# Five raw buffers, loads six blocks ahead, gate reads in four parts and a one-hot copied by ScalarE, in a decoder block with a 16,384-expert mixer

## The chip, the cores and the metric

The kernel runs on one core of a Trainium2 chip. The metric is the device time of one execution in microseconds. Three runs before the change took 1752.38, 1755.32 and 1758.9 us; the median is 1755.32 us. Of the two programs one execution more is profiled with the hardware profiler; that of the kernel before took 1750.83 us.

Engines are named as in the profile: PE (matrix multiply), DVE (VectorE), ACT (ScalarE), POOL (GpSimd), SP (SyncE, which issues most of the DMAs). Each works through its own list of instructions strictly in order.

## The reference

One decoder layer on 512 tokens of width 1024, in float32. The first half (state-space branch, sliding-window attention, gates, output projection) is not touched by the change. The second half is a product-key mixture of single-neuron experts:

```python
q = (xt @ w_query).reshape(t, PEER_HEADS, 2, PEER_KEY_DIM // 2)
s = jnp.einsum('thkd,hknd->thkn', q, sub_keys)
vals, idx = lax.top_k(s, PEER_TOPK)
cand = vals[:, :, 0, :, None] + vals[:, :, 1, None, :]      # 16 x 16 candidates per head
best, pos = lax.top_k(cand.reshape(t, PEER_HEADS, 256), PEER_TOPK)
expert = i1 * N_SUB_KEYS + i2                               # i1, i2 looked up by pos
gate = jax.nn.softmax(best, axis=-1)
a = einsum('cd,ced->ce', x, u_tab[expert])
w = gate * gelu(a)
out = einsum('ce,ced->cd', w, v_tab[expert])
```

Every token has 8 heads x 16 experts = 128 experts out of 16,384, and each expert is one row of 1024 numbers of the table `peer_u` and one of `peer_v`.

## The kernel before, in words

The kernel does the expert mixer in two ways at once.

**The dense way, for tokens 128 to 511.** Both tables are read whole, as 128 blocks of 128 experts each. A *U block* multiplies 128 rows of `peer_u` with the 384 tokens and applies gelu; a *V block* multiplies the weights (gelu times gate, zero where a token does not choose the expert) with 128 rows of `peer_v` and sums into six banks of PSUM that stay open to the end. Each product is made of three matrix products (`mm3`, and the like of it in `v_mm`): every float32 operand is split into a high part `hi` (cast to float32r on ACT, L123) and a low part `lo` (the difference, on DVE, L124), and hi·hi, hi·lo and lo·hi are summed. So a block of either table costs: one load of 512 KB into a `t_raw` buffer (issued by SP, L1120 or L1122), one cast on ACT, one subtraction on DVE, and 24 matmuls of 384 columns (`a_mm`, L93 to L95) or 18 of 512 columns (`v_mm`, L1156 to L1159) on PE. The result of a U block is evicted from PSUM by a gelu on ACT (L1132).

**The sparse way, for tokens 0 to 127.** `sparse_tile` gathers 256 rows, 128 of each table, with one expert per token in each gather (POOL, L1188, 512 KB each), and works each off on DVE in one instruction, L1205 for a row of `peer_u` and L1207 for one of `peer_v`. It is a generator that the main loop advances a little at each block.

**Gates.** Which expert a token takes is found on DVE (`topk`, for four tiles of 128 tokens). For the three dense tiles `gate_matrix` then makes the full table of gates, 384 tokens x 16,384 experts, as products of two one-hot matrices. For eight tokens at a time (a *gate step*, 48 in all) DVE makes four tiles of 128 x 1024 fp16: `ol` (which of 128 second indices, L1105), `oh` and `ol` (times the high and low part of the gate, L1106 and L1107) and `one` (which of 128 first indices, L1108). `ol`, `oh` hold the token as their innermost index; `one` holds it as the outer one, since its rows are what PE loads. One step later PE multiplies them (16 matmuls, L1091 and L1092), ACT evicts the result into `g_st`, and each 16 tokens ACT's queue writes 1 MB of `g_st` to the tensor `G_d` in DRAM. Later SP reads the gates of eight V blocks back in one DMA of 1536 KB (`v_g<-G_d`, L1136), two buffers in turn. All 24 writes of `G_d` come before the first of these reads.

**The order.** The table stages are one loop over `order`. Its first `ALONE` entries are U blocks, then V blocks come with the rest of the U blocks spread between them, one after about every third V block. As the list is built, one U block more stands ahead of the first V block, so 91 U blocks come first in the kernel before, and 37 U and 128 V blocks after. At place *i* the loop issues: the load of the block 4 places on (`table_load`), the split of the block 2 places on (`unit_split`), in the V stage also the read of gates, the read-back of a U result and the preparation of the weights (`w_prep`, L1145, L88, L89), then the block's matmuls, and then background work: `RATE_A` units of top-k and gate work (until it is done; it must be done ten blocks before `ALONE`), and `RATE_S` (before the V stage) or `RATE_V` (in it) units of the sparse way, 1.2 units to a row. DVE's and POOL's lists follow this order as it is written (`manual_schedule`). The lists of PE, ACT and SP are set by the framework's scheduler, which places instructions by its own estimate of when their inputs and buffers are free.

**Buffers.** Three `t_raw` buffers and three pairs `hi`/`lo` (`WB`). A load waits until the subtraction L124 has freed its buffer; a cast waits until PE has done with the `hi` of three blocks before. U results stay in SBUF while there is room: `RES` = 15 tiles `A_first`, and 20 tiles `A_mid` in the memory that the top-k frees tile by tile; the others go to DRAM (`A_d<-u_g`, L1353, issued by ACT, 192 KB) and come back in the V stage (`v_a<-A_d`, L1337, issued by SP). 54 of the 128 do.

**Semaphores of DMAs.** The framework hands out eight DMA semaphores in turn to every DMA that SP or ACT issues. A DMA whose semaphore was last given to another one waits, on the engine that issues it, until that other DMA has landed.

Of the kernel before, what the change touches and what calls it, by code (L numbers as in the profile page):

```python
# [10 lines left out]
F32 = mybir.dt.float32  # L11
# [47 lines left out]
class Builder:  # L59
    RATE_A, RATE_S, RATE_V, RATE_G = 2.4, 0.72, 1.44, 6.0  # L60
    ALONE = 90
    G0, S5C, G1, RATE_Q = 0, 70.0, 8.0, 3.0
# [6 lines left out]
    POOL_U, POOL_R = 2, (0,)  # L69
    RES, WB, SOLO = 15, (3, 3), 2.0  # L70

# [988 lines left out]
    def gate_matrix(self, pool, i12, gate, Gd, tile_no, cost=1.25):  # L1060
# [38 lines left out]
        for t1 in range(0, 128, TB):  # L1099
            tb = slice(t1, t1 + TB)  # L1100
            sh = [128, 128, TB]
            wide = lambda a: a[:, None, tb].to_broadcast(sh)
            oh, ol = (mk(sh, n, F16, bufs=2) for n in ("oh", "ol"))
            one = mk([128, TB, 128], "one", F16, bufs=2)
            nc.vector.tensor_tensor(ol, self.iota16, wide(iT[:, 1, :]), op=ALU.is_equal)  # L1105
            nc.vector.tensor_mul(oh, ol, wide(gh))  # L1106
            nc.vector.tensor_mul(ol, ol, wide(gl))  # L1107
            nc.vector.tensor_tensor(one, self.iota1[:, None, :].to_broadcast([128, TB, 128]),  # L1108
                                    iT[:, 0, tb, None].to_broadcast([128, TB, 128]), op=ALU.is_equal)
            if late:  # L1110
                multiply(*late)
            late = (t1, one, oh, ol)
            yield cost
        multiply(*late)

    def table_load(self, u):

        raw = self.wb.tile([128, D], F32, tag="raw", name=self.nm("t_raw"), bufs=self.WB[0])
        if u < 128:
            self.nc.sync.dma_start(out=raw.rearrange("p (k e) -> p k e", e=128), in_=self.i["peer_uT"][u])  # L1120
        else:
            self.nc.sync.dma_start(out=raw, in_=self.i["peer_v"][(u - 128) * 128:(u - 127) * 128, :])  # L1122
        return raw
# [9 lines left out]

    def g_load(self, pool, b, Gd):
        g = pool.tile([128, Gd.shape[0], self.GB, self.TS], F32, tag="v_g", name=self.nm("v_g"), bufs=2)
        self.nc.sync.dma_start(out=g, in_=Gd[:, :, b:b + self.GB, :].rearrange("g p b t -> p g b t"))  # L1136
        return g

# [72 lines left out]
    def run(self, out):  # L1211
# [4 lines left out]
        with ExitStack() as fs:  # L1216
# [86 lines left out]
            rows = L(fs, "rows")  # L1303
            A1 = L(fs, "ares1").tile([128, N1, DT], F32, name="A_first")
            free[:0] = [A1[:, n, :] for n in range(N1)]
            sparse = self.sparse_tile(sq, rows, xrow, ef0, gate0, hd[0], out[0])
# [13 lines left out]
            def ahead(i, n):  # L1320
                return order[i + n] if 0 <= i + n < len(order) else (2, 0)

            with tc.manual_schedule(engines={ET.DVE, ET.Pool}):
                for i in range(-4, len(order)):
                    v, b = ahead(i, 4)
                    if v < 2:
# [3 lines left out]
                    if vp:  # L1330
                        v, b = ahead(i, 8)
                        if v == 1 and b % self.GB == 0:
                            gg[b] = self.g_load(vp, b, Gd)
                        v, b = ahead(i, 4)
# [48 lines left out]
    def consts(self, pool):  # L1383
# [6 lines left out]
        self.iota16 = pool.tile([128, 128, 8], F16, name="iota16")  # L1390
        self.iota1 = pool.tile([128, 128], F16, name="iota1")
        nc.gpsimd.iota(self.iota1, pattern=[[1, 128]], base=0, channel_multiplier=0, allow_small_or_imprecise_dtypes=True)
        nc.gpsimd.iota(self.iota16, pattern=[[1, 128], [0, 8]], base=0, channel_multiplier=0, allow_small_or_imprecise_dtypes=True)
# [67 lines left out]
```

## Time and profile before

| | |
|---|---|
| median of three runs | 1755.32 us (1752.38 to 1758.9) |
| the profiled execution | 1750.83 us, of which the span of the trace is 1748.8 us |
| PE, DVE, ACT, POOL busy | 1631.2, 1444.8, 751.0, 580.2 us |
| first U block on PE | 527.4 us after the span's start |
| first V block on PE | 1038.4 us |
| 24 writes of `G_d`, 16 reads `v_g` | 1024 KB and 1536 KB each |
| mean DMA rate over the span | 243 GB/s |

Times in the views count from the span's start. A row of a group of instructions reads: line, engine, operation, output<-input, shapes, count, then busy time, the mean duration of one in ns, and the idle time of the engine just before, with what ended most of it. In the rows by stretch of time, each engine has its busy time and, in brackets, its number of instructions; then come the granted TensorE clock, the busy share of the DMA engines, and GB/s. In rows in order of time, the brackets at the end hold the idle time before the row and what ended it. "SPq" and "ACTq" are DMAs being issued on SP and ACT. Matmuls overlap in the trace (each starts before the one ahead has ended), so the pace of PE is read from the distance between starts.

### The profile page before, as it was taken

How to read it: one execution, taken by the hardware profiler on the slowest of the kernel's cores; microseconds unless marked ns; L12 is line 12 of the kernel's file. 1: busy time of each engine (PE TensorE's matmuls, PEld its weight loads, DVE VectorE, ACT ScalarE, POOL GpSimd, SP SyncE). 2: the span in 40 equal slices, each digit the busy share in tenths (PEclk: the TensorE clock that was granted, in tenths of full speed). 3: DMA queues.
4: the chain of work that ended last, by engine and by line, in shares of the span. 5: the costliest groups of instructions: out<-in, count | busy, mean ns of one | idle time of the engine just before them, and what ended most of it. 6: DMA issues, size and time to landing. Idle time of an engine off the chain costs nothing.

```text
span 1748.8 us, 24910 instructions
## 1 busy us (share of the span) xinstructions
PE 1631.2 (93%) x8831; PEld 1429.4 (82%) x8831; DVE 1444.8 (83%) x2931; ACT 751.0 (43%) x1242; POOL 580.2 (33%) x473
## 2 busy tenths in 40 slices
PE   7789999898999898898899799999999999999998
PEld 5568878786899888898889798888888888888776
DVE  6799778897798999999999467878777777778776
ACT  5256656565563434434444233333333333333332
POOL 2562123333521111111112143544444444444441
PEclk9899999999999999899999899999999999999999
DMA  7823452656744456666668988989999999999885
GB/s 227 150 85 97 151 169 84 169 164 190 232 138 164 161 207 235 223 223 238 243 227 303 348 302 299 313 314 322 330 328 340 320 321 334 336 323 324 285 289 195
DMA packets 231501, 424.10 MB, mean 243 GB/s; under 512 B 16160, under 2 KB 148304, under 8 KB 228304
## 3 DMA queue, kind: packets, MB, share of 16 engines
q1 hardware_dynamic: 171680, 237.97, 41.4%
q0 software_dynamic: 36864, 134.23, 21.2%
q10 hardware_dynamic: 22832, 50.30, 8.9%
q8 instruction: 69, 1.13, 0.3%
q14 instruction: 56, 0.46, 0.1%
HBM read 370.94 MB, written 51.51 MB: 242 GB/s over the span
## 4 chain that ended last, share of the span: by engine, by line
PE 45%; DVE 26%; DMA 8%; issue 4%; ACT 2%; SPq 2%; POOL 0%; ACTq 0%; DVEq 0%; POOLq 0%
PE po L1156 9%; PE po L1157 9%; PE po L1159 8%; DVE lo L124 6%; PE pa L93 4%; PE pa L95 4%; PE pa L94 4%; DMA t_raw<-peer_uT 3%; DVE g_one L1108 3%; DVE sp_row L1205 3%; DMA t_raw<-peer_v 2%; DVE g_oh L1106 2%; DVE g_ol L1105 1%; ACT hi L123 1%; SPq L1337 1%
## 5 line engine op out<-in xcount | busy, mean ns | idle before, releaser
L123 ACT CAST hi<-t_raw 128x1024 fp32r<-128x1024 f32 x256 | 269.1, 1051 | 461.4 <-PE pa L94 148.4
L93 PE MATMUL pa<-x2h,hi 128*128 128x384 f32 x1024 | 353.2, 345 | 36.9 <-ACT u_g L1132 25.8
L124 DVE TENSOR_TENSOR lo<-t_raw,hi 128x1024 fp32r<-128x1024 f32 x256 | 312.4, 1221 | 88.6 <-ACT hi L123 88.1
L1188 POOL DMA_INDIRECT sp_row<-peer_u,sp_ei x128 | 199.3, 1557 | 528.3 <-DVE sp_row L1205 489.0
L95 PE MATMUL pa<-x2h,lo 128*128 128x384 f32 x1024 | 349.2, 343 | 13.3 <-DVE lo L124 13.2
L94 PE MATMUL pa<-x2l,hi 128*128 128x384 f32 x1024 | 348.0, 340 | 0.0
L1156 PE MATMUL po<-hi,v_wh 128*128 128x512 f32 x768 | 304.6, 397 | 5.9 <-ACT v_wh L88 5.9
L1157 PE MATMUL po<-lo,v_wh 128*128 128x512 f32 x768 | 303.4, 395 | 0.0
L1188 POOL DMA_INDIRECT sp_row<-peer_v,sp_ei x128 | 195.6, 1528 | 273.2 <-DVE sp_acc L1207 240.9
L93 PEld LDWEIGHTS pa<-x2h,hi 128*128 128x128 f32 x1024 | 196.1, 192 | 47.1 <-ACT u_g L1132 29.7
L1159 PE MATMUL po<-hi,v_wl 128*128 128x512 f32 x768 | 228.7, 395 | 0.0
L95 PEld LDWEIGHTS pa<-x2h,lo 128*128 128x128 f32 x1024 | 195.8, 191 | 19.4 <-DVE lo L124 18.5
L94 PEld LDWEIGHTS pa<-x2l,hi 128*128 128x128 f32 x1024 | 196.1, 191 | 1.7
L1156 PEld LDWEIGHTS po<-hi,v_wh 128*128 128x128 f32 x768 | 144.3, 188 | 41.9 <-ACT v_wh L88 8.9
L1159 PEld LDWEIGHTS po<-hi,v_wl 128*128 128x128 f32 x768 | 143.8, 187 | 35.4
L1157 PEld LDWEIGHTS po<-lo,v_wh 128*128 128x128 f32 x768 | 144.3, 188 | 32.7
L1207 DVE SCALAR_TENSOR_TENSOR sp_acc<-sp_row,sp_a,sp_acc 128x1024 f32<-128x1024 f32 x128 | 163.7, 1279 | 1.0 <-DMA sp_row<-peer_v,sp_ei 0.7
L1205 DVE SCALAR_TENSOR_TENSOR sp_row<-sp_row,xrow 128x1024 f32<-128x1024 f32 x128 | 155.7, 1216 | 4.5 <-DMA sp_row<-peer_u,sp_ei 4.5
L89 DVE TENSOR_TENSOR v_wl<-v_w,v_wh 128x384 fp32r<-128x384 f32 x128 | 71.5, 558 | 103.2 <-ACT v_wh L88 103.2
L88 ACT CAST v_wh<-v_w 128x384 fp32r<-128x384 f32 x128 | 65.5, 512 | 211.2 <-DVE v_w L1145 211.0
L123 ACT CAST hi<-raw 128x1024 fp32r<-128x1024 f32 x88 | 92.0, 1048 | 87.0 <-PE gps L94 15.5
L124 POOL TENSOR_TENSOR lo<-raw,hi 128x1024 fp32r<-128x1024 f32 x28 | 70.0, 2499 | 117.3 <-ACT hi L123 117.3
(455 smaller groups left out, 2912.4 us busy)
## 6 DMA issues: line engine op xcount, KB each, us to landing
t_raw<-peer_uT SPq DMA_DIRECT2D x128, 512.0 KB, 4.3
t_raw<-peer_v SPq DMA_DIRECT2D x128, 512.0 KB, 4.9
G_d<-g_st ACTq DMA_DIRECT2D x24, 1024.0 KB, 5.7
v_g<-G_d SPq DMA_DIRECT2D x16, 1536.0 KB, 14.6
raw<-w_in SPq DMA_DIRECT2D x32, 512.0 KB, 4.2
A_d<-u_g ACTq DMA_DIRECT2D x54, 192.0 KB, 3.9
v_a<-A_d SPq DMA_DIRECT2D x54, 192.0 KB, 7.2
raw<-w_ab SPq DMA_DIRECT2D x64, 128.0 KB, 3.6
```

Source lines behind the costliest of these rows:

```text
L89: self.nc.vector.tensor_sub(lo, src, r32(hi))
L93: mm(out, lh, rh, start=first, stop=False)
L94: mm(out, lh, rl, start=False, stop=False)
L95: mm(out, ll, rh, start=False, stop=last)
L123: self.nc.scalar.copy(hi, raw)
L124: (self.nc.gpsimd if pool_lo else self.nc.vector).tensor_sub(lo, raw, r32(hi))
L1156: mm(po[j][i], wh[:, c], hi[:, hs[i]], start=first, stop=False)
L1157: mm(po[j][i], wh[:, c], lo[:, hs[i]], start=False, stop=False)
L1159: mm(po[j][i], wl[:, c], hi[:, hs[i]], start=False, stop=last)
L1188: nc.gpsimd.indirect_dma_start(out=got[k], out_offset=None, in_=self.i[n], in_offset=bass.IndirectOffsetOnAxis(ap=ei[:, s:s + 1], axis=0))
L1205: nc.vector.scalar_tensor_tensor(r, r, 1.0, xrow, op0=ALU.mult, op1=ALU.mult, accum_out=av[:, s:s + 1])
L1207: nc.vector.scalar_tensor_tensor(acc, r, av[:, s:s + 1], acc, op0=ALU.mult, op1=ALU.add)
```

## The change

- `table_load` takes its buffers from two pools: of every five loads in turn three go to the old three buffers and two to a new pool `wx` with two. Loads are issued six places ahead (`FAR`), where it was four.
- To make room, `RES` falls from 15 to 9. 68 U results go through DRAM where 54 did.
- The read of gates for eight V blocks is issued as four DMAs of 384 KB (`PARTS`), 8, 7, 6 and 5 places ahead of their first use, where it was one DMA of 1536 KB 8 places ahead.
- `one` is made in two steps: DVE makes `o1` with the token innermost (as `ol` is), and ACT copies it into `one` with the token as the outer index.
- `ALONE` is 96 where it was 90, and the rates of the background work are 2.2, 0.96 and 1.36 where they were 2.4, 0.72 and 1.44 (`RATE_A`, `RATE_S`, `RATE_V`).
- The constant `iota1` goes.

```diff
-    RATE_A, RATE_S, RATE_V, RATE_G = 2.4, 0.72, 1.44, 6.0
-    ALONE = 90
+    RATE_A, RATE_S, RATE_V, RATE_G = 2.2, 0.96, 1.36, 6.0
+    PARTS = 4
+    ALONE, MORE, FAR = 96, 2, 6
...
-    RES, WB, SOLO = 15, (3, 3), 2.0
+    RES, WB, SOLO = 9, (3, 3), 2.0
...
             one = mk([128, TB, 128], "one", F16, bufs=2)
+            o1 = mk(sh, "o1", F16, bufs=2)
+            nc.vector.tensor_tensor(o1, self.iota16, wide(iT[:, 0, :]), op=ALU.is_equal)
+            nc.scalar.copy(one, o1.rearrange("p b t -> p t b"))
             nc.vector.tensor_tensor(ol, self.iota16, wide(iT[:, 1, :]), op=ALU.is_equal)
             nc.vector.tensor_mul(oh, ol, wide(gh))
             nc.vector.tensor_mul(ol, ol, wide(gl))
-            nc.vector.tensor_tensor(one, self.iota1[:, None, :].to_broadcast([128, TB, 128]),
-                                    iT[:, 0, tb, None].to_broadcast([128, TB, 128]), op=ALU.is_equal)
...
-        raw = self.wb.tile([128, D], F32, tag="raw", name=self.nm("t_raw"), bufs=self.WB[0])
+        self.loads += 1
+        pool, n = (self.wb, self.WB[0]) if self.loads % (self.WB[0] + self.MORE) < self.WB[0] else (self.wx, self.MORE)
+        raw = pool.tile([128, D], F32, tag="raw", name=self.nm("t_raw"), bufs=n)
...
-    def g_load(self, pool, b, Gd):
-        g = pool.tile([128, Gd.shape[0], self.GB, self.TS], F32, tag="v_g", name=self.nm("v_g"), bufs=2)
-        self.nc.sync.dma_start(out=g, in_=Gd[:, :, b:b + self.GB, :].rearrange("g p b t -> p g b t"))
-        return g
+    def g_load(self, g, b, Gd, part):
+        n = Gd.shape[0] // self.PARTS
+        q = slice(part * n, part * n + n)
+        self.nc.sync.dma_start(out=g[:, q], in_=Gd[q, :, b:b + self.GB, :].rearrange("g p b t -> p g b t"))
...
+            self.wx, self.loads = L(fs, "wx"), -1
...
-                for i in range(-4, len(order)):
-                    v, b = ahead(i, 4)
+                for i in range(-self.FAR, len(order)):
+                    v, b = ahead(i, self.FAR)
...
-                        v, b = ahead(i, 8)
-                        if v == 1 and b % self.GB == 0:
-                            gg[b] = self.g_load(vp, b, Gd)
+                        for part in range(self.PARTS):
+                            v, b = ahead(i, 8 - part)
+                            if v == 1 and b % self.GB == 0:
+                                if part == 0:
+                                    gg[b] = vp.tile([128, Gd.shape[0], self.GB, self.TS], F32, tag="v_g", name=self.nm("v_g"), bufs=2)
+                                self.g_load(gg[b], b, Gd, part)
```

What the change makes of the engines' lists is seen at three places. Line numbers after L1066 differ by a few between the two programs; a name ends in the program's number of the tile, and a higher number was written later.

**SP around the first reads of gates.** Before, 81 loads of table blocks (U0 to U80) stand ahead of these rows' first read; the first three rows are the loads of U78, U79 and U80, and the last is that of U81:

```order
L1120 DMA t_raw_10598<-peer_uT 128x1024
L1120 DMA t_raw_10635<-peer_uT 128x1024
L1120 DMA t_raw_10672<-peer_uT 128x1024
L1136 DMA v_g_10943<-G_d 128x24x128
L1136 DMA v_g_11348<-G_d 128x24x128
L1337 DMA v_a_12284<-A_d 128x384
L1337 DMA v_a_12313<-A_d 128x384
L1337 DMA v_a_12392<-A_d 128x384
L1337 DMA v_a_12427<-A_d 128x384
L1120 DMA t_raw_10709<-peer_uT 128x1024
```

In the changed program the first rows are the loads of U86 and U87, and the last is that of U90:

```order
L1124 DMA t_raw_10969<-peer_uT 128x1024
L1124 DMA t_raw_11009<-peer_uT 128x1024
L1141 DMA v_g_11314<-G_d 128x6x128 x2
L1124 DMA t_raw_11046<-peer_uT 128x1024
L1141 DMA v_g_11314<-G_d 128x6x128 x2
L1141 DMA v_g_11692<-G_d 128x6x128 x2
L1124 DMA t_raw_11083<-peer_uT 128x1024
L1141 DMA v_g_11692<-G_d 128x6x128 x2
L1345 DMA v_a_12108<-A_d 128x384
L1345 DMA v_a_12140<-A_d 128x384
L1345 DMA v_a_12217<-A_d 128x384
L1345 DMA v_a_12494<-A_d 128x384
```

88 loads now stand ahead of the first read, and the loads of U88 and U89 stand between its parts. Later in the V stage the four parts of a read stand one behind another in SP's list, with no load between them.

**SP at the start of the table stages.** Before, loads stand in the order of the blocks, U0 first. In the changed program (from U0 on):

```order
L1124 DMA t_raw_5992<-peer_uT 128x1024
L1124 DMA t_raw_5994<-peer_uT 128x1024
L1124 DMA t_raw_5996<-peer_uT 128x1024
L1124 DMA t_raw_6006<-peer_uT 128x1024
L1124 DMA t_raw_6012<-peer_uT 128x1024
L1124 DMA t_raw_6052<-peer_uT 128x1024
L1124 DMA t_raw_5998<-peer_uT 128x1024
L1124 DMA t_raw_6000<-peer_uT 128x1024
L1124 DMA t_raw_6093<-peer_uT 128x1024
```

The loads of U5, U6 and U7 (tiles 6006, 6012, 6052, in the old buffers of U0, U1 and U2) stand ahead of those of U3 and U4 (tiles 5998 and 6000, in the new pool).

**DVE at a gate step.** Before, four instructions, the last of them L1108:

```order
L124 TENSOR_TENSOR lo_9612<-t_raw_9487,hi_9611 128x1024
L1105 TENSOR_TENSOR g_ol_9642<-iota_66,g_iT_9592 128x1024
L1106 TENSOR_TENSOR g_oh_9641<-g_ol_9642,g_gh_9596 128x1024
L1107 TENSOR_TENSOR g_ol_9642<-g_ol_9642,g_gl_9597 128x1024
L1108 TENSOR_TENSOR g_one_9643<-iota_67,g_iT_9592 128x1024
```

In the changed program also four, and `g_o` (the tile `o1`) comes first and reads the same kind of operands as `g_ol`:

```order
L125 TENSOR_TENSOR lo_9947<-t_raw_9717,hi_9946 128x1024
L1107 TENSOR_TENSOR g_o_1828_9979<-iota_66,g_iT_9887 128x1024
L1109 TENSOR_TENSOR g_ol_9977<-iota_66,g_iT_9887 128x1024
L1110 TENSOR_TENSOR g_oh_9976<-g_ol_9977,g_gh_9891 128x1024
L1111 TENSOR_TENSOR g_ol_9977<-g_ol_9977,g_gl_9892 128x1024
```

Counted in DVE's list from the subtraction of U0 to the last one-hot of the last gate step: before, 74 subtractions and 40 sparse rows (36 of L1205, 4 of L1207) stand there; after, 80 and 59 (46 and 13). From there to the first V block's weights there are 21 sparse rows before and 19 after, and 195 and 178 from there to the end.

More of the change, by code (lines that the diff above doesn't have):

```diff
@@ L1390, in consts @@
         self.iota16 = pool.tile([128, 128, 8], F16, name="iota16")
-        self.iota1 = pool.tile([128, 128], F16, name="iota1")
-        nc.gpsimd.iota(self.iota1, pattern=[[1, 128]], base=0, channel_multiplier=0, allow_small_or_imprecise_dtypes=True)
         nc.gpsimd.iota(self.iota16, pattern=[[1, 128], [0, 8]], base=0, channel_multiplier=0, allow_small_or_imprecise_dtypes=True)
```

## The prediction

> **What bounds the kernel now.** I read first the busy times by stretch, cut at the first subtraction of a table block (521.6 us), the last one-hot (948.4), the first V block (1038.4) and the last matmul (1742.7). The front half ends before these and is left as it is.
>
> ```profile
> core 0: us, PE busy (x) PEld busy (x) DVE busy (x) ACT busy (x) POOL busy (x), PEclk, DMA share, GB/s
> 521.60:948.40 426.80, 387.46 (x2576) 367.14 (x2576) 409.79 (x1058) 180.94 (x271) 71.14 (x44) 0.98 0.61 219
> 948.40:1038.40 90.00, 78.19 (x442) 77.00 (x441) 51.13 (x58) 27.23 (x39) 26.58 (x22) 0.94 0.95 329
> 1038.40:1742.70 704.30, 696.28 (x3193) 586.60 (x3192) 548.36 (x695) 246.82 (x330) 297.18 (x190) 1.00 0.89 311
> ```
>
> Three stretches with three limits. In the first, A, DVE is busy 409.8 of 426.8 us: it makes top-k, gates, splits and sparse rows, and sets the pace. In the third, C, PE does. The second, B, is the switch, where DMA stands at 0.95 and no engine is full.
>
> What PE itself needs is read from distances between starts: the six `L1159` of a V block return each 4.20 us, the gelus of a U block each 4.16 us where nothing waits, and the matmuls of a gate step stand 0.06 us apart, 1.0 us for 16.
>
> ```profile
> 1728.88 1.40 PE po L1159 x6
> 1733.08 1.40 PE po L1159 x6
> 1001.95 0.48 ACT L1132 ACTIVATE u_g<-pa 128x384 f32<-128x384 f32 x1
> 1006.11 0.48 ACT L1132 ACTIVATE u_g<-pa 128x384 f32<-128x384 f32 x1
> 940.65 0.23 PE L1091 MATMUL pg<-g_one,g_oh 128*128 128x128 f16 x1
> 940.71 0.22 PE L1092 MATMUL pg<-g_one,g_ol 128*128 128x128 f16 x1
> ```
>
> How many blocks each stretch holds is the count of L93 (eight to a U block) and L1156 (six to a V block), for B and C; in A the subtractions L124 are counted.
>
> ```profile
> 948.40:1038.40 90.00, 48.51 (x141) 27.19 (x140) 0.94 0.95 329
> 1038.40:1742.70 704.30, 99.55 (x296) 55.56 (x296) 1.00 0.89 311
> 1038.40:1742.70 704.30, 304.60 (x768) 144.16 (x768) 1.00 0.89 311
> 521.60:948.40 426.80, 89.94 (x74) 78.86 (x75) 0.98 0.61 219
> ```
>
> C: 296/8 + 768/6 = 165 blocks x 4.2 = 693.0 of 704.3 us, so 11.3 us of stall. B: 141/8 = 17.6 blocks x 4.16 + 1.0 for the last gate step = 74.3 of 90.0, so 15.7 us of stall. A: 74 blocks x 4.16 + 48 = 355.8 us of PE work in 426.8, so PE has 71 us to spare there.
>
> Where B's stall comes from, the ACT and SP lists in order of time tell:
>
> ```profile
> 968.35 0.49 ACT L1132 ACTIVATE u_g<-pa 128x384 f32<-128x384 f32 x1 [1.80 <-DMA A_d<-u_g]
> 980.30 0.33 ACTq L1353 DMA_DIRECT2D A_d<-u_g  x1
> 981.04 1.04 ACT L123 CAST hi<-t_raw 128x1024 fp32r<-128x1024 f32 x1 [12.20 <-DMA v_g<-G_d]
> 958.85 0.33 SPq L1120 DMA_DIRECT2D t_raw<-peer_uT  x1
> 965.27 9.53 SPq L1136 DMA_DIRECT2D v_g<-G_d  x2
> 974.84 8.48 SPq L1337 DMA_DIRECT2D v_a<-A_d  x4
> 983.42 2.98 SPq L1120 DMA_DIRECT2D t_raw<-peer_uT  x3
> ```
>
> Two things stand in line. SP issues no load from 958.9 to 983.4 us: it waits for the last write of `G_d` (until 965.2), then issues the gate reads for 9.5 us and four read-backs for 8.5. And ACT, whose write `A_d` takes the DMA semaphore that the first gate read holds, is kept from 968.8 to 980.3, with the next cast and gelu behind it.
>
> **The change, part by part.**
>
> (1) *Six blocks more ahead of the first V block* (97 for 91). C has 159 blocks for 165: 6 x 4.2 = **-25.2 us**. What it costs in A is six more splits, below.
>
> (2) *DVE's work in A.*
>
> ```profile
> L124 DVE TENSOR_TENSOR lo<-t_raw,hi 128x1024 fp32r<-128x1024 f32 x256 | 312.4, 1221 | 88.6 <-ACT hi L123 88.1
> L1207 DVE SCALAR_TENSOR_TENSOR sp_acc<-sp_row,sp_a,sp_acc 128x1024 f32<-128x1024 f32 x128 | 163.7, 1279 | 1.0 <-DMA sp_row<-peer_v,sp_ei 0.7
> L1205 DVE SCALAR_TENSOR_TENSOR sp_row<-sp_row,xrow 128x1024 f32<-128x1024 f32 x128 | 155.7, 1216 | 4.5 <-DMA sp_row<-peer_u,sp_ei 4.5
> L1108 DVE TENSOR_TENSOR g_one<-iota,g_iT 128x1024 f16<-128x1024 f16 x48 | 58.4, 1217 | 0.0
> L1105 DVE TENSOR_TENSOR g_ol<-iota,g_iT 128x1024 f16<-128x1024 f16 x48 | 32.7, 682 | 0.5 <-PE pg L1092 0.3
> L123 ACT CAST hi<-t_raw 128x1024 fp32r<-128x1024 f32 x256 | 269.1, 1051 | 461.4 <-PE pa L94 148.4 <-PE po L1159 111.5 <-DMA t_raw<-peer_uT 81.6
> DVE lo L124 <- ACT hi L123: 3.2, 2, 2.2
> ACT hi L123 <- PE pa L94: 103.0, 35, 6.0
> ```
>
> The last two rows are waits within A: total us, times, longest.
>
>
> `one` took 1217 ns, `o1` has the operands of L1105, 682 ns: 48 x 0.535 = -25.7. By DVE's list A then holds six more splits (6 x 1.22 = 7.3) and 19 more sparse rows, ten of L1205 and nine of L1207 (12.2 + 11.5 = 23.7). Sum **+5.3**: what the one-hot saves is spent on sparse rows moved out of C. There they were under PE's cover, so C gains nothing for them.
>
> (3) *The copy on ACT.* 48 copies of 1024 elements; the nearest row is the cast L123, 1.05 us, so 50 us on an engine that works 181 of A's 427. Hidden, if ACT does it while it would wait for PE; not hidden, if casts come later for it. Bounds 0 and 50.4.
>
> (4) *How near PE comes to DVE.* A will hold 80 x 4.16 + 48 = 381 us of PE work beside 415 of DVE's, and the copies of (3) lie between them. Single steps are uneven and only two split blocks lie between the engines, so now one, now the other waits. DVE idles 17.0 us in A with PE 71 us below the stretch; with 51 us I scale, 17.0 x 71/51 = 23.7, and take **+7** for (3) and (4) together, the nearer to the low end because DVE waits for ACT's casts only 3.2 us of A now, and they for PE 103. The bounds are 0 and 50.
>
> (5) *U3 and U4 behind U7 in SP's list.* The load of U7 needs the buffer of U2, free when U2's subtraction ends, and so the load of U3 is no earlier:
>
> ```profile
> 527.91 1.22 DVE L124 TENSOR_TENSOR lo<-t_raw,hi 128x1024 fp32r<-128x1024 f32 x1 [2.21 <-ACT hi L123]
> 534.75 1.22 DVE L124 TENSOR_TENSOR lo<-t_raw,hi 128x1024 fp32r<-128x1024 f32 x1
> t_raw<-peer_uT SPq DMA_DIRECT2D x128, 512.0 KB, 4.3
> v_g<-G_d SPq DMA_DIRECT2D x16, 1536.0 KB, 14.6
> v_a<-A_d SPq DMA_DIRECT2D x54, 192.0 KB, 7.2
> ```
>
> U2's subtraction ends at 529.1. Some 2 us later (its new memory also waits for the query's last products), then 4.3 to land and 1.05 for the cast: 536.5 or so, where DVE wants U3 at 534.75. DVE's list is fixed, so it waits: **+2.5**, bounds 0 and 5.
>
> (6) *B.* The last write of `G_d` took 10.41 us, the reads of both buffers 14.6 in the median and 19.8 at most (the second row: least, median, most):
>
> ```profile
> 954.78 10.41 DMA G_d<-g_st
> DMA to landing us min/median/max: 11.2/14.6/19.8
> ```
>
> At the last gate write PE has seven loaded blocks ahead where it had six, and loads of two more stand between the parts of the reads. What is late next is ACT: the write of U84's result takes the semaphore of the first read-back `v_a`, which stands behind all eight parts. From the last write of `G_d` (issued near the start of U81) the row times give 10.4 us to land, 16.6 until the first read-back is issued (965.3 to 981.9), and 3 to 7 to land: 30 to 34. ACT comes to that write after four blocks, 16.6; PE can do two blocks more into its two PSUM buffers, 8.3. That leaves 5 to 9 us; I take 6 for 15.7, **-9.7**. Bounds: 0 and 15.7 left.
>
> (7) *C's stall.* Its longest single piece is a late load:
>
> ```profile
> 1413.80 1.04 ACT L123 CAST hi<-t_raw 128x1024 fp32r<-128x1024 f32 x1 [8.14 <-DMA t_raw<-peer_uT]
> PE po L1156 <- ACT v_wh L88: 5.9, 6, 1.6
> PE pa L93 <- ACT hi L123: 2.0, 1, 2.0
> ```
>
> Two more buffers give a load two blocks more, 8.4 us, which covers 8.14. The six short waits for the weights are an order of ACT's list and stay. **-4.3**, to 7 of 11.3; bounds 2 and 15 left. Reads in four parts do little here, for they stand one behind another.
>
> (8) *Fourteen more results through DRAM*: 14 x 192 KB written and read; in C +2.7 MB, against 17 rows and 6 loads fewer, -12 MB. Nothing, at 0.89; uncovered it would be 2.7 MB at 311 GB/s, 9 us. Removing `iota1`: one POOL instruction before the first matmul, nothing.
>
> Sum: -25.2 + 5.3 + 7 + 2.5 - 9.7 - 4.3 = **-24.4 us**, from 1750.8 to 1726.4. The median of the runs lies 4.5 above that execution, so I forecast **1731** for a median.
>
> The Trainium skill speaks against (6): "DMA: Bandwidth & Descriptors", section "Bandwidth", wants 1 MiB or more in a DMA for 75% of peak, and the parts have 384 KB. The trace of C agrees little: most of its DMAs are of 512 KB, and the engines stand at 0.89. What the rule would do here is rival 3.
>
> **Rivals.**
>
> *1. The blocks move, but the switch stays.* The parts queue as one read does, SP and ACT are held as long, and C keeps its stalls: without (6) and (7) the change is -24.4 + 14.0 = -10.4, **1745**. For it: ACT waits for a semaphore still. Against: two loads stand between the parts.
>
> *2. PE and DVE get in each other's way in A.* The term (4) is 25 for 7: -6.4, **1749**. For it: 381 of 432 us PE. Against: DVE idles 4% now.
>
> *3. Slower: small gate reads land late.* A read-back of 192 KB takes 7.2 us and a read of 1536 KB 14.6, so by the straight line through these 384 KB take 8.3; if the eight parts land one after another, 66 us pass where 16.6 did. ACT's write in (6) then waits 50 us longer: 1731 + 50 = **1781**. It decides from 24 us on, that is from 5 us a part. Against: both reads together, 3 MB, landed within 19.8 us.
>
> *4. Slower: the copy joins the loop cast, subtraction, matmul, free buffer.* All 48 copies on the path: 50.4 for 7, +19, **1774**; it decides from 31.4/48 = 0.65 us a gate step. For it: ACT's list is in order, and copies stand right ahead of casts. Against: ACT is 42% busy in A, and its casts wait mostly for PE.
>
> **How the numbers follow.** Chances: forecast 0.62, rival 1 0.18, rival 2 0.10, rival 3 0.03, rival 4 0.07. A measurement here tells 0.5%, about 9 us, from no change: faster is under 1746.5, slower over 1764. Forecast, 0.62, and most of rival 1, 0.16, are faster: 0.78; the rest of it and rival 2 are the same: 0.12; rivals 3 and 4 slower: 0.10. Low bounds of all terms (A +5.3 alone, B no stall, C 2 us left) give -25.2 + 5.3 - 15.7 - 9.3 = -44.9 from 1755.3, 1710; I begin there and end at 1755, past rivals 1 and 2. The forecast's own range is 1710 to 1745.
>
> **What would show it.** (1) The first V block near 1041 to 1046 us, at most some us later than now, with 97 U blocks before it, and C near 675 us. (2) A group `g_o` of 48 x 682 ns, and DVE over 95% busy in A. (3) A copy of about 1.05 us; PE's gate matmuls not waiting for it. (5) DVE waiting some us for U3's cast at 535. (6) ACT waiting for a read-back's semaphore, 15 us or so, with PE idle 6. (7) No cast waiting 8 us for a load in C. I am wrong if the first V block comes after 1070, or if C takes over 690.

## The result and the profile after

The changed kernel takes **1728.6 us** in the median of four runs (1727.2 to 1729.6), the kernel before 1754.6 us (1752.4 to 1758.9): a ratio of 0.985 with a 95% interval of 0.983 to 0.987. The profiled execution took 1727.2 us with a span of 1725.4, 23.6 us less than that of before. Forecast were 1731 us, range 1710 to 1755, and 24.4 us less for the execution. The sum came out right. Several of its terms did not, and their errors nearly cancel.

The same three stretches, cut at the same events (in the profile of after lines stand one to eight further down):

```profile
core 0: us, PE busy (x) PEld busy (x) DVE busy (x) ACT busy (x) POOL busy (x), PEclk, DMA share, GB/s
521.40:952.90 431.50, 403.88 (x2694) 387.30 (x2694) 411.57 (x1090) 277.07 (x326) 103.92 (x63) 0.98 0.71 251
952.90:1047.60 94.70, 81.20 (x468) 79.92 (x467) 51.22 (x57) 31.31 (x43) 24.52 (x22) 0.93 0.92 316
1047.60:1718.90 671.30, 668.09 (x3050) 560.75 (x3048) 524.45 (x663) 240.39 (x319) 258.67 (x173) 1.00 0.88 311
```

A went from 426.8 to 431.5 us, B from 90.0 to 94.7, C from 704.3 to 671.3. A ends with the last one-hot of the first indices (`one` before, `o1` now). Before, that is the last of a gate step's four instructions on DVE; now it is the first, and the other three, 2.1 us, fall into B. To the end of that gate step A is 433.6 us long. DVE still paces A (411.6 of 431.5), with PE now close behind it (403.9).

The groups of the new one-hot (the copy's name `g_o` is `o1`):

```profile
L1107 DVE TENSOR_TENSOR g_o<-iota,g_iT 128x1024 f16<-128x1024 f16 x48 | 32.8, 684 | 0.0
L1108 ACT COPY g_one<-g_o 128x1024 f16<-128x1024 f16 x48 | 98.9, 2063 | 14.0 <-DVE g_o L1107 10.1 <-DVE lo L125 1.5 <-ACT g_st L1095 0.8
```

Three rows of the waits within A (total, times, longest):

```profile
ACT hi L124 <- PE pa L95: 120.6, 58, 5.5
DVE lo L125 <- ACT hi L124: 5.1, 3, 2.2
PE pg L1092 <- ACT g_one L1108: 1.7, 4, 0.8
```

`o1` takes 684 ns as priced. The copy takes 2063 ns, twice the 1.05 us that was taken for it, and is hidden all the same: PE waits 1.7 us in all for a copy, and ACT's casts, with ACT busy 277 of 431.5 us, still wait 120.6 us for PE.

What holds B is the same kind of wait as before, now on another DMA. ACT's list there in order of time:

```profile
961.12 0.33 ACTq L1097 DMA_DIRECT2D G_d<-g_st  x1
...
976.88 1.06 ACT L124 CAST hi<-t_raw 128x1024 fp32r<-128x1024 f32 x1 [2.91 <-PE pa L96]
980.61 1.04 ACT L124 CAST hi<-t_raw 128x1024 fp32r<-128x1024 f32 x1 [2.67 <-PE pa L95]
981.56 0.48 ACT L1136 ACTIVATE u_g<-pa 128x384 f32<-128x384 f32 x1
995.41 0.33 ACTq L1361 DMA_DIRECT2D A_d<-u_g  x1
995.85 1.04 ACT L124 CAST hi<-t_raw 128x1024 fp32r<-128x1024 f32 x1 [13.81 <-DMA v_a<-A_d]
996.80 0.48 ACT L1136 ACTIVATE u_g<-pa 128x384 f32<-128x384 f32 x1
```

SP's list beside it, and the row of what PE waits for in B, first after and then before the change:

```profile
971.68 1.12 SPq L1141 DMA_DIRECT2D v_g<-G_d  x2
...
987.61 4.26 SPq L1345 DMA_DIRECT2D v_a<-A_d  x4
991.99 15.11 SPq L1124 DMA_DIRECT2D t_raw<-peer_uT  x5
```

```profile
PE pa L94 <- ACT u_g L1136: 13.5, 3, 10.8
```

```profile
PE pa L93 <- ACT u_g L1132: 11.8, 3, 9.2
```

The last write of `G_d` is issued at 961.1, the first read-back at 987.6, and ACT's `A_d` write, which has to wait for that read-back's semaphore, passes at 995.4, 34.3 us after the first of the three. The gelu behind it ends at 997.3, and the 10.8 us that PE waits for it begin at 986.5. The pause costs more than its own length: the block after it takes PE 7.2 us instead of 4.16, and the granted clock from 997.3 to 1006.0 is 0.65. Before the change the block after the 9.2 us took 7.1.

In C two waits for cast weights are left, where before there were six and one for a late load (rows of waits within C, total, times, longest):

```profile
PE po L1160 <- ACT v_wh L89: 3.2, 2, 1.6
```

### The profile page after: what moved, and what is told of

Same layout as the page of the kernel before. It is cut to its first block, busy times and chain, and to the rows that moved or that the text cites. A ratio compares the mean times of both kernels' runs of the same rounds, so it can differ in the third digit from the quotient of the medians.

```text
span 1725.4 us, 25152 instructions
## 1 busy us (share of the span) xinstructions
PE 1625.8 (94%) x8831; PEld 1429.5 (83%) x8831; DVE 1426.2 (83%) x2931; ACT 844.4 (49%) x1290; POOL 571.4 (33%) x472
## 4 chain that ended last, share of the span: by engine, by line
PE 60%; DVE 18%; DMA 3%; ACT 3%; issue 3%; POOL 0%; SPq 0%; DVEq 0%; ACTq 0%; POOLq 0%
PE po L1160 10%; PE po L1161 10%; PE po L1163 10%; PE pa L94 7%; PE pa L96 7%; PE pa L95 6%; DVE lo L125 4%; DVE sp_row L1209 2%; ACT hi L124 1%; DVE g_oh L1110 1%; DVE t_s L966 1%; DMA gl<-g_d 1%; DVE g_o L1107 1%; DVE g_ol L1109 1%; DVE t_ix L968 1%
## 5 line engine op out<-in xcount | busy, mean ns | idle before, releaser
L1192 POOL DMA_INDIRECT sp_row<-peer_u,sp_ei x128 | 188.4, 1472 | 417.7 <-DVE sp_row L1209 379.2
L96 PEld LDWEIGHTS pa<-x2h,lo 128*128 128x128 f32 x1024 | 195.1, 191 | 16.5 <-DVE lo L125 15.7
```

The costliest lines, as they stand in the source:

```text
L96: mm(out, ll, rh, start=False, stop=last)
L1192: nc.gpsimd.indirect_dma_start(out=got[k], out_offset=None, in_=self.i[n], in_offset=bass.IndirectOffsetOnAxis(ap=ei[:, s:s + 1], axis=0))
```

## The experiments

All are edits of the changed kernel. Each runs beside the kernel before on its chip, whose medians there were 1752.4 to 1756.2 us. "Ratio" is to those runs. A, B and C are the stretches in each profiled execution; the stall of C is its length less 159 blocks (165 with the old pacing) of 4.2 us, that of B its length less 4.16 us for each block and 1.0 for each gate step in it. By this count B's stall is 15.7 us before and 17.5 after the change; two gate steps lie in it now, where one did. Most of it is PE standing idle (11.8 before, 13.5 after), and some 3 us in each are the slow block after the longest pause.

| kernel | median us (range) | ratio, 95% interval | A | B | C |
|---|---|---|---|---|---|
| before | 1754.6 (1752.4–1758.9) | | 426.8 | 90.0 | 704.3 |
| after | 1728.6 (1727.2–1729.6) | 0.985 (0.983–0.987) | 431.5 | 94.7 | 671.3 |
| u_one | 1752.0 (1749.5–1756.4) | 0.998 (0.996–1.000) | 456.8 | 92.2 | 671.2 |
| u_bufs | 1726.4 (1726.1–1732.6) | 0.983 (0.980–0.985) | 438.3 | 92.7 | 673.7 |
| u_parts | 1726.9 (1726.0–1727.8) | 0.983 (0.980–0.985) | 432.9 | 93.8 | 671.1 |
| u_pace | 1728.6 (1728.2–1730.4) | 0.988 (0.985–0.991) | 403.9 | 95.9 | 700.1 |
| u_rows | 1736.5 (1731.8–1739.7) | 0.988 (0.985–0.991) | 416.2 | 97.4 | 693.7 |
| rows_act | 1699.9 (1698.1–1701.2) | 0.971 (0.968–0.974) | 416.4 | 87.5 | 667.3 |
| act_c | 1716.9 (1714.8–1718.5) | 0.979 (0.974–0.983) | 431.8 | 86.9 | 667.3 |
| late | 1720.1 (1718.4–1723.2) | 0.983 (0.980–0.986) | 431.6 | 86.1 | 671.2 |
| best1 | 1697.1 (1695.6–1698.4) | 0.968 (0.964–0.972) | 416.3 | 84.6 | 667.3 |
| best2 | 1691.7 (1690.7–1693.2) | 0.965 (0.961–0.969) | 402.6 | 84.2 | 667.5 |
| best3 | 1681.9 (1681.2–1682.7) | 0.959 (0.956–0.961) | 402.7 | 83.0 | 667.6 |

The kernel `copy` has a single time, 1809.5 us.

### Which part made it faster: the four parts undone one at a time

**The one-hot** (u_one):

```diff
-            o1 = mk(sh, "o1", F16, bufs=2)
-            nc.vector.tensor_tensor(o1, self.iota16, wide(iT[:, 0, :]), op=ALU.is_equal)
-            nc.scalar.copy(one, o1.rearrange("p b t -> p t b"))
+            nc.vector.tensor_tensor(one, self.iota1[:, None, :].to_broadcast([128, TB, 128]),
+                                    iT[:, 0, tb, None].to_broadcast([128, TB, 128]), op=ALU.is_equal)
```

> The changed kernel, with the token-order one-hot made by DVE again (1217 ns for 682 ns, 48 times, 25.7 us more of DVE work in the first stretch) and no copy on ACT. If DVE sets the pace of the first stretch, as the prediction's terms (2) to (4) have it, that stretch grows from 431.6 to about 455 us and the run comes to about 1752. The rival, that PE, busy 404 of these 432 us, is by now as near to the bound as DVE, and that the copies of 2.06 us hold the loop up, has the stretch grow by 5 to 12 us only: 1734 to 1741.

Measured: 1752.0 us, the theory's number. A in its rows by stretch:

```profile
524.00:980.80 456.80, 415.62 (x2725) 392.63 (x2724) 438.89 (x1093) 188.58 (x283) 103.72 (x63) 0.98 0.69 240
```

DVE does 27.3 us more and A is 25.3 us longer; 2.1 us of both are the cut's, so like for like it is 25.3 us of work and 23.2 of time. ACT does 88.5 us less and nothing gets shorter for it. DVE paces A, and the copies are free at 2.06 us each. Undoing this one edit takes back 23.4 of the 26 us that the change won; with all the other edits in, the ratio is 0.998 (0.996 to 1.000).

**The buffers** (u_bufs; `RES` stays at 9):

```diff
-    ALONE, MORE, FAR = 96, 2, 6
+    ALONE, MORE, FAR = 96, 0, 4
```

> The changed kernel with three raw buffers and loads four blocks ahead, as before the change; parts, copy and pacing stay. By terms (5) and (7): U3's wait in the first stretch goes (2 us less), and late loads come back into the third stretch, whose stall goes from 3.6 to 11 us or so: 1733 to 1737. The rival, that the third stretch lost its stall through the reads in parts alone, gives 1727 to 1730.

Measured: 1726.4 us, just under the rival's range, though not for the rival's reason: with whole reads (u_parts, next) C is as short. C's stall is 5.9 us for 3.5, with three gaps of PE for two. The five buffers save 2.4 us there and cost 2.0 in A, where U3 is late (DVE's list of the changed kernel),

```profile
536.59 1.23 DVE L125 TENSOR_TENSOR lo<-t_raw,hi 128x1024 fp32r<-128x1024 f32 x1 [1.98 <-ACT hi L124]
```

so that nothing is left of them. That the buffers do what they say is plain from ACT's waits in C, first of u_bufs, then of the changed kernel:

```profile
ACT hi L124 <- DMA t_raw<-peer_v: 71.1, 19, 6.8
```

```profile
ACT hi L124 <- DMA t_raw<-peer_v: 2.1, 3, 0.9
```

The casts came late 71 us in all, but PE had two split blocks in hand and felt 2.4 of them. (The profiled execution of u_bufs is the one of 1732.6 us, and its A of 438.3 is part of what made it longer than its three sisters. DVE waits there 3.6 us longer for ACT's `g_iT` and 3.7 longer for PE's gate products than in the changed kernel; why these came later is open.)

**The parts** (u_parts):

```diff
-    PARTS = 4
+    PARTS = 1
```

> The changed kernel with each gate read as one DMA again, buffers, copy and pacing stay. The switch has as much stall with the parts (17 us) as without them before the change (15.7), so the parts may be worth nothing there: 1727 to 1732, with ACT held by the gate read's own semaphore again. The rival, that the parts did shorten ACT's wait and other changes made it longer, gives 5 to 10 us of stall more in the switch, 1734 to 1739.

Measured: 1726.9 us; B's stall 16.6 us with whole reads, 17.5 with parts. The parts are worth nothing, and cost nothing either: DMA moved 319 GB/s in B with reads of 1536 KB and 316 with 384 KB.

**The pacing** (u_pace):

```diff
-    RATE_A, RATE_S, RATE_V, RATE_G = 2.2, 0.96, 1.36, 6.0
+    RATE_A, RATE_S, RATE_V, RATE_G = 2.4, 0.72, 1.44, 6.0
-    ALONE, MORE, FAR = 96, 2, 6
+    ALONE, MORE, FAR = 90, 2, 6
```

> The changed kernel with the old pacing (90 blocks ahead of the first V block, the old three rates); buffers, parts and the copy on ACT stay. By terms (1) and (2) the first stretch does six splits and 19 sparse steps less and comes to about 400 us (431.6 less 31), the third has six blocks more: 696 to 704 us. That is 1721 to 1729, so that the new pacing is worth nothing and the whole gain is the one-hot's 25.7 us. The rival, that the pacing carries the gain as term (1) counts it, gives 1745 to 1755. The stall of the third stretch tells besides whether buffers or pacing shortened it: 4 to 7 us if the buffers did, 9 or more if the pacing did.

Measured: 1728.6 us, the median of the changed kernel to a tenth.

```profile
520.40:924.30 403.90, 378.03 (x2546) 359.56 (x2546) 382.60 (x1055) 268.33 (x314) 71.07 (x44) 0.99 0.66 234
924.30:1020.20 95.90, 81.35 (x472) 80.07 (x471) 52.96 (x60) 31.67 (x44) 27.35 (x22) 0.93 0.94 320
1020.20:1720.30 700.10, 693.70 (x3193) 585.87 (x3192) 551.41 (x695) 248.59 (x330) 295.19 (x190) 1.00 0.90 316
```

What PE waits for in its C:

```profile
PE po L1160 <- ACT v_wh L89: 6.4, 4, 1.6
```

The new pacing puts 27.6 us into A and takes 28.8 out of C and 1.2 out of B; in the medians nothing is left of that. C's stall, though, is 7.1 us here: the old pacing with the new buffers stands between 11.3 (before) and 3.5 (after). Buffers, parts and copy together took 4.2 us of it, pacing the other 3.6, as four waits for cast weights became two.

### Why the pacing touches C's stall

The next run moves sparse steps the other way, out of A into C.

```diff
-    RATE_A, RATE_S, RATE_V, RATE_G = 2.2, 0.96, 1.36, 6.0
+    RATE_A, RATE_S, RATE_V, RATE_G = 2.2, 0.72, 1.54, 6.0
```

> The changed kernel with fewer sparse rows between the table blocks before the switch (the first stretch holds 38 and 6 of their two steps for 46 and 13, 18.7 us of DVE work less; the third holds 12 steps more). If DVE sets the pace of the first stretch and the third is PE's, the first goes from 431.6 to about 415 us and the third stays: 1711 to 1716. The rival, that PE is the bound of the first stretch too by now, gives a gain of 0 to 6 us: 1722 to 1728. A third stretch that grows by more than 3 us would say that its DMA share, 0.88 already, is the bound there.

Measured: 1736.5 us, slower than either expectation. A did as the theory said, 15.3 us shorter. C, which was thought to be covered by PE, is 22.4 us longer:

```profile
522.70:938.90 416.20, 398.10 (x2692) 382.02 (x2691) 394.15 (x1067) 277.36 (x326) 77.59 (x48) 1.00 0.70 242
938.90:1036.30 97.40, 81.59 (x470) 80.16 (x469) 54.13 (x62) 31.05 (x43) 29.25 (x24) 0.91 0.95 325
1036.30:1730.00 693.70, 673.31 (x3050) 561.89 (x3048) 534.39 (x684) 235.38 (x318) 294.58 (x185) 1.00 0.88 311
```

The DMA share over C is 0.88, as in the changed kernel, and DVE is busy 77%. What PE waits for there:

```profile
PE po L1160 <- ACT v_wh L89: 18.0, 12, 1.8
PE pa L94 <- ACT hi L124: 2.4, 2, 1.2
```

One such place, first in DVE's list in order of time, then in ACT's:

```profile
1590.88 2.60 DVE L1211 SCALAR_TENSOR_TENSOR sp_acc<-sp_row,sp_a,sp_acc 128x1024 f32<-128x1024 f32 x2
1593.40 1.22 DVE L125 TENSOR_TENSOR lo<-t_raw,hi 128x1024 fp32r<-128x1024 f32 x1
1594.53 0.55 DVE L1149 TENSOR_TENSOR v_w<-A_first,v_g 128x384 f32<-128x384 f32 x1
1598.60 0.56 DVE L90 TENSOR_TENSOR v_wl<-v_w,v_wh 128x384 fp32r<-128x384 f32 x1 [3.52 <-ACT v_wh L89]
```

```profile
1592.91 1.05 ACT L124 CAST hi<-t_raw 128x1024 fp32r<-128x1024 f32 x1 [2.54 <-PE po L1163]
1597.11 1.04 ACT L124 CAST hi<-t_raw 128x1024 fp32r<-128x1024 f32 x1 [3.15 <-PE po L1163]
1598.07 0.51 ACT L89 CAST v_wh<-v_w 128x384 fp32r<-128x384 f32 x1
```

The weights `v_w` are ready at 1595.1. ACT is idle then, but its next entry is not `v_wh`: it is the cast `hi` of a later block, which waits until PE ends its block and gives a buffer back. PE ends at 1597.0, needs `v_wh` for the very next block, and waits for the cast and for `v_wh`: 1.05 and 0.51, 1.6 us. DVE's list is the program's, ACT's is the scheduler's. Where DVE has two sparse steps in a row `v_w` comes later, and the likely reason for the order is that the scheduler estimated it later than the cast. Counted in the lists of instructions, the weights' cast stands behind the casts of two later blocks (such places), and the gaps of 1.2 to 1.8 us of PE in C are:

```
kernel      such places   gaps of PE in C
before           3          3 of 1.6 us (and others, one of 2.0 for a load)
after            2          2
u_bufs           1          3
u_pace           4          4
u_rows          14         14
rows_act         0          0
```

Two explanations were left: this order, or DVE and the DMA engines being full, for DVE's work and its waits for `v_wh` (534 and 143 us) together nearly fill C (694). The next run decides. It is u_rows with ACT's list, too, in the order of the program from the switch on:

```diff
-            with tc.manual_schedule(engines={ET.DVE, ET.Pool}):
+            with tc.manual_schedule(engines={ET.DVE, ET.Pool}), ExitStack() as man:
...
                         vp = L(fs, "vp", side="right")
+                        man.enter_context(tc.manual_schedule(engines={ET.DVE, ET.Pool, ET.Activation}))
```

> The kernel with fewer sparse rows before the switch (u_rows), with ACT's list after the switch in the order of the program instead of the planner's, so that a cast of weights v_wh never stands behind a later block's cast. In u_rows 14 of 128 stood behind two later casts, and PE waited 14 times for 1.2 to 1.8 us. If that order made u_rows' third stretch 22 us longer, it goes from 693.7 to 671 to 680 us: 1713 to 1722. The rival, that DVE, whose work and waits for v_wh together fill the stretch, or the DMA engines, at 0.98 there, are the bound, leaves it at 688 to 695: 1730 to 1738.

Measured: 1699.9 us, below even the theory's range, for B became shorter too.

```profile
938.70:1026.20 87.50, 81.38 (x471) 79.25 (x470) 53.20 (x60) 32.15 (x43) 32.12 (x24) 0.96 1.01 358
1026.20:1693.50 667.30, 667.30 (x3049) 560.23 (x3047) 541.83 (x685) 239.38 (x318) 269.68 (x185) 1.00 0.92 324
```

PE has no idle time in C at all, with the same sparse steps at the same rate. The order of ACT's list is the cause of u_rows' loss; that the planner's estimate of `v_w` made this order is argued, not shown. B is 9.9 us shorter besides. The same edit without fewer sparse rows (act_c):

> The changed kernel with nothing else than ACT's list after the switch in the order of the program. If the 1.59 us gaps of the third stretch come from weights cast behind two later blocks, both go: 671.2 to 667 or 668 us. In the switch the gelu stands ahead of the next cast then, so that PE gets a result buffer back before ACT waits for a semaphore: stall from 18.5 to 9 to 12 us, as in rows_act. Together 1714 to 1721. The rival, that rows_act was fast through its pacing and not its order, leaves 1725 to 1730.

Measured: 1716.9 us, B 86.9 and C 667.3, as the theory said. (The 18.5 us of the expectation count one gate step in B, the 17.5 here two; by the latter count it fell to 9.7.)

### What stalls the switch

```diff
-    PARTS = 4
+    PARTS, LATE = 4, 8
...
                         vp = L(fs, "vp", side="right")
+                        A2 = vp.tile([128, self.LATE, DT], F32, name="A_late")
+                        free.extend(A2[:, n, :] for n in range(self.LATE))
```

> The changed kernel with eight more tiles on chip for results of the U blocks, opened at the switch, so that U81 to U88 are not written to DRAM and ACT issues no A_d write while the gate reads stand in line. If ACT's A_d write behind the first read-back is what stalls PE there (term (6)), the 17 us go to 0 to 3 and the run comes to 1711 to 1716. The rival, that the casts themselves would have waited for SP's late loads anyway, leaves 9 to 17 us of stall: 1720 to 1729.

Measured: 1720.1 us, at the lower end of the rival's range; B's stall is 8.9 us for 17.5. The direction is the theory's, the size half of it. The rival's reason is not seen: the casts below wait for PE, not for loads. What is left in ACT's list:

```profile
960.96 0.36 ACTq L1097 DMA_DIRECT2D G_d<-g_st  x1
964.00 1.04 ACT L124 CAST hi<-t_raw 128x1024 fp32r<-128x1024 f32 x1 [3.07 <-PE pa L95]
969.63 0.87 ACT L1136 ACTIVATE A_late<-pa 128x384 f32<-128x384 f32 x2 [4.59 <-DMA G_d<-g_st]
976.67 1.05 ACT L124 CAST hi<-t_raw 128x1024 fp32r<-128x1024 f32 x1 [6.18 <-PE pa L95]
```

The wait for a read-back's semaphore is gone. In its place the first result waits for the last write of `G_d`: the new tiles lie in the memory of `g_st`, which that write still reads. That wait is the experiment's own. So `A_d` writes that stand behind SP's reads make at least 8.6 of B's 17.5 us.

act_c takes nearly as much out of B (17.5 to 9.7) and keeps the `A_d` writes. Its order of ACT's list gives PE a result buffer back between two shorter waits of the writes, of 6.4 and 7.0 us, where one of 13.8 stood. The two put together, with fewer rows in A (best1 is rows_act and late):

> rows_act with the eight tiles of late. If ACT's A_d writes cause what stall is left in the switch (10.9 us), 4 to 8 us of it go: 1692 to 1696. The rival, that in this order the writes no longer matter because the gelu stands ahead of the casts, gives 1697 to 1702.

Measured: 1697.1 us, B 84.6 for 87.5. That is the rival's number, at its edge: in this order the eight tiles still save something, but 3 us, not 8. How much the writes themselves cost there stays open, since the only wait of PE that is left in best1's B, 4.3 us for the first result in the new tiles, is again the tiles' own.

### The copy's own price

```diff
-            nc.scalar.copy(one, o1.rearrange("p b t -> p t b"))
+            nc.scalar.copy(one.rearrange("p t b -> p b t"), o1)
```

> The changed kernel with ACT's copy of the one-hot walking its source in order of addresses and writing with the stride, where it read with the stride. If the strided read makes the 2.06 us, the copy falls to 1.0 to 1.1 us, as the cast of the same size takes; the rival, that a stride on either side costs the same, leaves it at 2.06. The time stays within 3 us of 1728 either way, since ACT is not the bound.

Measured: neither. The group in its profile, A, and the row of what PE waits for (total, times, longest, from 521 to 1010 us):

```profile
L1108 ACT COPY g_one<-g_o 128x1024 f16<-128x1024 f16 x48 | 233.6, 4877 | 4.3 <-ACT g_st L1095 1.6 <-ACT u_g L1136 0.8 <-DVE sp_row L1209 0.4
520.80:1029.00 508.20, 416.85 (x2665) 403.72 (x2665) 416.16 (x1089) 395.64 (x320) 96.73 (x63) 0.93 0.60 213
PE pg L1092 <- ACT g_one L1108: 62.1, 37, 3.5
```

The copy takes 4.88 us when it writes with the step (256 bytes between neighbours) and 2.06 when it reads with one (16 bytes). The steps differ, so the sides are not compared at equal step. With 2.8 us more for each copy A is 76.7 us longer, and no engine is full in it: ACT is busy 395.6 of 508.2 us, DVE 416, PE 417. PE waits 62.1 us for the copies, where in the changed kernel it waited 1.7. This is rival 4 at work, copies that stand on PE's path. At 2.06 us a copy it does not show; at 4.88 it costs 1.6 us a gate step.

### A version that beats both

best2 is best1 with `RATE_S` 0.48 and `RATE_V` 1.5, and in C the product `v_w` stands ahead of the subtraction `lo` in DVE's list, so that ACT makes `v_wh` while DVE subtracts. What that order is worth by itself was not measured:

```diff
+                    v, b = ahead(i, 2)
+                    if vp and v == 1 and b in as_:
+                        ws[b] = self.w_mul(vp, as_.pop(b), gg[b - b % self.GB][:, :, b % self.GB, :])
                     if ahead(i, 2)[0] < 2:
                         parts[ahead(i, 2)] = self.unit_split(raws.pop(ahead(i, 2)))
...
-                            ws[b] = self.w_prep(vp, as_.pop(b), gg[b - b % self.GB][:, :, b % self.GB, :])
+                            if b not in ws:
+                                ws[b] = self.w_mul(vp, as_.pop(b), gg[b - b % self.GB][:, :, b % self.GB, :])
+                            ws[b] = self.w_split(vp, ws[b])
```

> best1 with 15 sparse steps fewer in the first stretch (18.7 us less of DVE work there), these steps in the third, and there the product v_w ahead of the subtraction lo in DVE's list, so that DVE no longer waits for the cast v_wh (75 us in rows_act). If the first stretch is near PE's bound (398 us busy in rows_act), it goes from 416 to 404 to 408 us, and the third stays at 667 to 670, with the DMA share near 0.96: 1681 to 1688. The rival, that the DMA engines are the bound of the third stretch by then, has it grow by as much as the first loses: 1693 to 1700.

Measured: 1691.7 us, between the two. A (402.6) is a little shorter than the theory has it and C as it has it, but from the last matmul to the end 13.1 us pass where best1 needs 4.5, since DVE still had sparse steps to do. best3 sets `RATE_V` to 1.6 and changes nothing else:

> best2 with the sparse steps of the third stretch set 0.1 us a block denser, so that the last of them ends before the last matmul: in best2 DVE still had nine of them behind the last subtraction and 13.1 us passed from the last matmul to the end, where best1 needed 4.5. If the third stretch bears the rate, that tail goes back to 4.5 to 6.6 us and the run comes to 1683 to 1687. The rival, that DVE or the DMA engines are full at this rate, gives gaps of PE in the third stretch, which eat the gain: 1689 to 1695.

Measured: **1681.9 us**, a ratio of 0.959 to the kernel before (0.956 to 0.961), 46.7 us below the changed kernel, and lower than the theory's range.

```profile
521.50:924.20 402.70, 391.53 (x2671) 379.99 (x2670) 376.29 (x1042) 275.18 (x322) 52.71 (x33) 0.99 0.66 231
924.20:1007.20 83.00, 81.90 (x491) 80.96 (x490) 55.97 (x66) 33.91 (x48) 31.71 (x24) 1.00 1.00 358
1007.20:1674.80 667.60, 667.60 (x3050) 560.74 (x3048) 549.05 (x705) 232.90 (x318) 260.72 (x199) 1.00 0.93 331
```

PE is now first in all three stretches: 391.5 of 402.7, 81.9 of 83.0, and all of C.

## Why the prediction was right, and where it was not

**In one line**, by the forecast's terms for the profiled execution:

| term | forecast | measured |
|---|---|---|
| (1) six blocks out of C | −25.2 | −25.2 |
| (2) to (5) A, like for like | +14.8 | +7.7 |
| (6) stall of B | −9.7 | +1.8 |
| (7) stall of C | −4.3 | −7.8 |
| sum | −24.4 | −23.5 |

A itself grew 4.7 us; half a block and one gate step (3.0 us of PE) fell behind its end cut, hence 7.7. The executions differ by 23.6.

**(1)** was right as arithmetic. As a gain it is none: the six blocks go into A, and u_pace shows the whole pacing to be worth 0. The forecast's own terms said that, −25.2 against 7.3 + 23.7 for splits and rows. The change gains what the one-hot saves DVE, and u_one shows it alone.

**(2)** has the right sizes: `o1` 684 ns, DVE 413.6 us to the end of the last gate step for 415 forecast. One sentence in it failed, that C gains nothing from the 19 rows which leave it, "under PE's cover". The rows' time was covered; their place in DVE's list was not, for ACT's planned list changed with it. By u_pace the pacing is worth 3.6 us of C's stall, by u_rows and rows_act 22 us where it goes the other way.

**(3) and (4)** were mis-sized on both sides. The copy costs 98.9 us on ACT, nearly twice the bound of 50.4 that was to hold it, and the coupling taken at 7 us was under 1: DVE idles 19.9 us in A for 17.0, and U3's wait is 2.0 of the difference. The price came from a cast that reads its values side by side, which the copy does not. The row that speaks for a small (4) was quoted, ACT's casts waiting 103 us for PE: idle time of that kind was room for the copies. Scaling DVE's idle time by PE's spare time had no mechanism behind it. **(5)** was right, 2.0 us for 2.5.

**(6) failed.** It was the term with the most reasoning in it, and most of its steps held. ACT's `A_d` write waited for the first read-back as described and passed 34.3 us after the last write of `G_d`, just over the 30 to 34 that were worked out. PE did the six blocks that it was given for that time and stood still 25.4 us after that write (at 986.5), where 24.9 were forecast. Two steps were wrong. The wait does not end with the write: a cast and the gelu stand behind it, so PE gets its buffer back only at 997.3, 36.2 us after, and 36.2 less 25.4 is the 10.8 us that took the place of 6. And these 6 us of one wait were set against the whole stall of 15.7, of which the like wait was only 9.2 (the row of before above). Two waits of 1.3 us and the slow block of some 3 us beside it were put at nothing for after, and they stayed. Like for like the forecast was 9.2 to 6, and 9.2 to 10.8 came of it. late shows that the writes cause at least 8.6 us of B's 17.5, act_c that another order of ACT's list takes out nearly as much with the writes kept. The two overlap, for best1 has only 2.9 us less B than rows_act.

**(7)** was right for the buffers, 4.2 us of C's stall by u_pace (its profile against that of before, which holds the copy and the parts as well). The late load itself held PE 2.0 us, and the 36 matmuls behind that pause took 1.8 us longer than their pace. The term was wrong in "an order of ACT's list and stay": the order is what the pacing changed.

**The rivals.** Rival 1 was half true: the switch stayed as it was, C did not. Rival 2 fell, with PE and DVE both over 93% busy in A. Rival 3, small reads that land late, fell with u_parts: B moved 316 GB/s with reads of 384 KB and 319 with 1536 KB. The Trainium skill ("DMA: Bandwidth & Descriptors", section "Bandwidth") asks for 1 MiB or more in a DMA for 75% of peak. The two rates in B show no difference that would bear it out. Rival 4 did not come at 2.06 us a copy; at 4.88 the copies put 1.6 us a gate step on the path, over the 0.65 from which it was to decide.

That the total came within 2.4 us of the median rests on errors of +7.1, −11.5 and +3.5 us in the terms that nearly cancel, and the median lies 1.4 us above the profiled execution where 4.5 were added. That is luck. The forecast of the sign rests on one term that was sound, DVE's work in the stretch that DVE paces.

## What to carry to other kernels

Work moved from an engine that paces a stretch to one that waits there can be worth nearly its full time (25.3 us of work gave 23.2 here), even where it costs 2.06 us there and saves 0.53 here; work moved between two stretches that are both near their bound is worth nothing until the stalls are counted. Where some engines' lists follow the program and another's is planned, a change of pacing can reorder the planned one too (2, 4 and 14 such places here): look in its list for an instruction that is ready and stands behind one that is not. When many waits of one length recur (here 1.6 us, a cast of 1.05 and one of 0.51), look for an order before a bandwidth.

## What was not expected of the hardware

ACT copies 128 x 1024 fp16 values in 2.06 us when it reads them 16 bytes apart and in 4.88 us when it writes them 256 bytes apart; the cast of as many float32 values side by side takes 1.05 us.

The DMA engines were taken for nearly full at a share of 0.89 in C. best3 ran C at 0.93 and 331 GB/s, and its B at 1.00 and 358 GB/s, without PE waiting for a load in either.

A pause of PE can cost more than its length; most of the short ones here did not. The pace of matmuls is 0.17 us in a U block (4.16 us for 24) and 0.23 in a V block (4.2 for 18). In C the 36 matmuls after a pause of 1.59 us take 0.1 to 0.3 us longer than by this pace. After the late load before the change, a pause of 1.99 us, they take 1.8 us longer (granted clock 0.70 from 1416.0 to 1420.0), after one of 1.79 us in u_rows 2.0, and after the 10.8 us in B of the changed kernel 3.2. What decides between the two cases was not measured: in act_c only 0.6 us follow a pause of 1.91.
